# Six DRAM copies moved behind a weight reload, one product's low part moved last, one head's keys loaded map by map

## The chip, the cores and the metric

The kernel runs on one core of one Trainium2 chip. The metric is the device time of one execution in microseconds (us). A core has five engines with a queue of instructions each: TensorE (PE, matmuls and transposes), VectorE (DVE), ScalarE (ACT), GpSimd (POOL) and SyncE (SP), which here only issues DMA transfers. An engine takes its queue in order; semaphores hold an instruction until what it reads is there.

## The reference

One layer of a hybrid decoder, sequence 1024, width 1024, all in fp32. The normalised input `h` is multiplied by one wide matrix; the columns of the product feed differential attention (8 heads, each with two maps of queries and keys of width 64) and gated linear attention (GLA, 4 heads); both results are gated, multiplied by `w_out`, normalised, and added to `x`.

```
h = rms_norm(x, pre_g)
z = h @ w_in
qa, ka, va, ga, qb, kb, vb, gb, gk_low = split_columns(z)
oa = diff_attention(qa, ka, va, lam)      # per block: w = softmax(q1 k1^T) - lam softmax(q2 k2^T); w @ v
oa = rms_norm(oa, subln_g) * (1 - lam_init) * silu(ga)
ob = gla_chunked(qb, kb, vb, log_sigmoid(gk_low @ w_gk_up + b_gk) / 16)
ob = rms_norm(ob, gla_g) * silu(gb)
y = concat([oa, ob]) @ w_out
return x + rms_norm(y, post_g)
```

## The kernel before, in words

**Arithmetic.** TensorE multiplies in a reduced fp32 format, so an operand that must keep its precision is split into a high part (a rounded copy, made by ACT as a CAST) and a low part (the rest, made by DVE as a subtraction). A product is three groups of matmuls that add up in one PSUM bank: high times high, high times low, low times high.

**The first stage** computes `h @ w_in` by pairs of column blocks, each with a seven-product scheme of the Strassen kind on 2 by 2 blocks of h (h11, h12, h21, h22) and of the weights (b11, b12, b21, b22). Products are numbered 1 to 7. Product 1 uses h11, 2 h12, 3 s4, 4 h22, 5 s1, 6 s2, 7 s3, where s1 to s4 are sums and differences of blocks of h. `order` (L270 on) lists steps (pair p, product n). Pairs 0 and 1, called GATED, are the value columns of GLA: they come first, both with the same weights tiles but other columns of h. Step (p, n) works for two units, 128 rows of the output each. So (0, 1) and (1, 1) come first, then (0, 2) and (1, 2), then two steps of pair 2, then (0, 5), (1, 5), (0, 6), (1, 6), (0, 7), (1, 7), (0, 4), (1, 4).

`multiply_values` (L455 to L472) issues such a step. For p in GATED, h is the stationary operand and the weights stream. For n below 3 each unit's chain stands alone: four matmuls with h high and w high (`y<-w,h_hi`), four with h low and w high (`y<-w,h_lo`), four with h high and w low. A weight tile of product n covers two of the four slices k of the inner dimension, so a product has two high tiles and two low tiles.

`step_values` (L548) follows each step with what drains it. After product 6 ACT copies bank x to a tile s (`s<-x`, four copies named s_785, s_787, s_823, s_825 for the four units). After products 2, 4 and 3 DVE adds a bank and such a tile into gv_st (`take_gated`, L523), frees the bank, and two stores of 128 KB on SP's queue (L528) write it out. gv_st has four buffers.

`gated_weights` (L321) makes the weights of a product: DVE subtracts raw blocks (`g_raw<-g_raw`), ACT casts the high part (`w<-g_raw`), DVE subtracts for the low part (`w<-g_raw,w`). The raw blocks are loaded on SP's queue by `load_gated` (L257) and, since b21 is needed a second time when its buffers have been overwritten, by `load_again` (L261 to L266), twice, 512 KB each, into g_raw_651 and g_raw_752. Raw weights of later pairs come through `load_raw` (L218) as w_raw. `parts` (L751) makes the high and low parts of s1, s2, s3, s4, h22 from fp32 tiles t.

After step (1, 4) the main flow computes the low-rank gate input (`low_rank`, L929): PSUM tile gkl_ps takes a bank that a gv_st of the product 2 or 4 stage has freed.

**Attention** runs later, head by head (its score matmuls `sc` stand at 615.8 to 885.4 us). `all_scores` (L1365) walks the query blocks qb from 7 to 0; after block 4 of a head it calls `load_qk` (L1143) for the next head: queries q, keys k and keys with halves exchanged ks, for half 1 and half 0 of the sequence, each map a DMA of 256 KB (q, k, L1152) or two of 128 KB (ks, L1155). `turn` (L1389) transposes the weights of the softmax difference on PE into `wtr`.

**The output stage** `out_early` (L1573) accumulates parts of the final product. At its top of the loop over st, six copies move rows of x into the output, DRAM to DRAM, 16 x 8192 elements or 512 KB each (L1589), to which the last stage adds its result (a DMA with `accum_op`).

**Order.** PE's instructions are pinned to the order of the program. All other engines' instructions are put in order when the program is built, by a scheduler that goes by its own times (`schedule_with_timeline_sim`), within the data dependencies and `tc.issue_after(a)`, which puts what is issued in its scope behind instruction a. The six copies depend on nothing but their input, and the scheduler puts them near the start of SP's queue.

Of the kernel before, what the change touches and what calls it, by code (L numbers as in the profile page):

```python
# [14 lines left out]
P = 128  # L15
# [10 lines left out]
QA, KA, VA, GA, QB, KB, VB, GB, GKL = 0, 1024, 2048, 3072, 4096, 4608, 5120, 6144, 7168  # L26
# [5 lines left out]
def hymba_kernel(  # L32
# [21 lines left out]
    pe, sp = nc.tensor, nc.sync  # L54
# [22 lines left out]
    def fp(t):  # L77
        return t.bitcast(F32)

    def cols(half):  # L80
        return slice(half * 512, half * 512 + 512)
# [61 lines left out]
    def mm(*a, **k):  # L143
        tc.keep_in_program_order(pe.matmul(*a, **k))  # L144
# [25 lines left out]
    def at(part, j):  # L170
        per = HB // len(part)
        return part[j // per][:, j % per]
# [31 lines left out]
    GATED = (0, 1)  # L204
# [45 lines left out]
    def load_gated(name):  # L250
# [4 lines left out]
        for i, r in enumerate(gated_raws[name]):  # L255
            rows = slice(r0 + i * 256, r0 + i * 256 + 256)
            sp.dma_start(r, w_in[0, rows, c0 : c0 + 512].rearrange("(k p) c -> p k c", p=P))  # L257
            if name == "b11" and not i:
                sp.dma_start(pre_g, pre_norm_g[0].rearrange("(k p) -> p k", p=P))

    def load_again(i):  # L261

        r = kp.tile([P, 2, 512], F32, tag=("ks0", "k0")[i], name="g_raw")
        gated_raws.setdefault("b21x", []).append(r)
        rows = slice(512 + i * 256, 512 + i * 256 + 256)
        sp.dma_start(r, w_in[0, rows, VB : VB + 512].rearrange("(k p) c -> p k c", p=P))  # L266

    EARLY = 3
    order = [(0, 1), (1, 1), (0, 2), (1, 2), (2, 1), (2, 2)]
# [185 lines left out]
    def multiply_values(i, pss, start):  # L455

        p, n = order[i]
        hi, lo = H[LEFT[n]]
        w = ws.pop(i)
        def chains(us):  # L460
            for j, (a, b) in enumerate(((0, hi), (0, lo), (1, hi))):
                for k in range(HB):
                    for u in us:
                        c = (p % 2 * 2 + u) * P
                        mm(
                            pss[u], at(b, k)[:, c : c + P], w[a][k // 2][:, k % 2, :],
                            start=(start and j == 0 and k == 0), stop=(j == 2 and k == HB - 1),
                            skip_group_check=True,
                        )

        for us in ((0,), (1,)) if p in GATED and n < 3 else ((0, 1),):
            chains(us)  # L472
# [667 lines left out]
        for st in streams:  # L1140
            yield from st

    def load_qk(h, n, half):  # L1143

        if h % 2 and half == 0 and n != "q":
            t = smps[0].tile([P, 2, 512], F32R, tag=f"{n}0", name=f"{n}0")
        else:
            t = kp.tile([P, 2, 512], F32R, tag=f"{n}{half}", name=f"{n}{half}")
        for m in range(2):
            d = qk_d["q" if n == "q" else "k"][h][m, :, :, cols(half)]  # L1150
            if n != "ks":
                ins = sp.dma_start(fp(t[:, m]), d.rearrange("t p s -> (t p) s"))  # L1152
            else:
                for i in range(2):
                    ins = sp.dma_start(fp(t[64 * i : 64 * i + 64, m]), d[1 - i])  # L1155
        qk_load[:] = [ins.ins]
        qk[h, n, half] = t

    qk, smps, qk_load = {}, [], []
# [8 lines left out]
    for n in ("q", "k", "ks"):  # L1168
        load_qk(0, n, 1)
        if n != "q":  # L1170
            load_qk(0, n, 0)
# [28 lines left out]
    def mix(st):  # L1200

        part = mix_tiles()
        for t in range(2):
            ins = (pool if st == 1 else sp).dma_start(fp(part[t]), mixe[st, t])
            if st < 2:
                tc.keep_in_program_order(ins)
        return part
# [157 lines left out]
    def all_scores():  # L1365
        for h in range(DA_HEADS):
            for qb in range(NT - 1, -1, -1):
                if qb in (3, 5) and h:
                    yield lambda h=h, half=qb // 4: (h - 1, half) in used
                yield from scores(h, qb)  # L1370
                if qb == 4 and h + 1 < DA_HEADS:
                    for n in ("q", "k", "ks"):
                        load_qk(h + 1, n, 1)
                    late = qk_load[0]
                    for n in ("k", "ks"):
                        load_qk(h + 1, n, 0)
                    for t in range(0 if h else 2):
                        with tc.issue_after(late):
                            sp.dma_start(fp(v_first[t])[:, 4:], v_d[0][0, t][:, 4:])
            if h + 1 < DA_HEADS:  # L1380
                load_qk(h + 1, "q", 0)
        scored.append(True)
        opened.update(dict.fromkeys(SC))
# [144 lines left out]
    def load_mix(st, e, n, pool_d=None):  # L1528
        rows = slice(st * P, (st + 1) * P)
        if pool_d:  # L1530
            raw = pool_d.tile([P, 4, P], F32, tag="m_raw", name="m_raw", bufs=4)
        else:
            raw = wop.tile([P, 4, P], F32, tag="m_raw", name="m_raw", bufs=4)
        mix_load[:] = [sp.dma_start(raw[:, :n, :], md[:, e : e + n, rows]).ins]
        return raw
# [20 lines left out]
    def times(ps, part, e0, dh, e, last):  # L1556
        mh, ml = part
        hi, lo = wo[e]
        for i, (a, b) in enumerate(((mh, hi), (ml, hi), (mh, lo))):
            mm(  # L1560
                ps, a[:, e - e0, :], b[:, cols(dh)],
                start=(e == e0 and i == 0), stop=(e == last and i == 2),
            )

    def y_bank(st, dh, name):
        return bank(Y[dh], [P, 512], name)

    def y_tile(ps):
        y = smp.tile([P, 512], F32, tag="yst", name="yst", bufs=2)
        act.copy(y, ps)  # L1570
        return y

    def out_early():  # L1573

        part = mix0
        ps = [y_bank(0, dh, "ypart") for dh in range(2)]
        for e in range(E, E + 8):
            yield 1.0
            if e == E:
                nxt = mix1  # L1580
            for dh in range(2):
                times(ps[dh], part, E, dh, e, E + 7)
            yield 1.0
        for dh in range(2):
            sp.dma_start(yd[0][dh], y_tile(ps[dh]))
        for st in range(1, NT - 1):
            part, nxt = nxt, mix(st + 1)
            rows = slice(ENDS[st - 1] * P, ENDS[st - 1] * P + P)
            sp.dma_start(out[0, rows, :], x[0, rows, :])  # L1589
            for dh in range(2):  # L1590
                ps = y_bank(st, dh, "ypart")
                for e in range(E, E + 8):
                    times(ps, part, E, dh, e, E + 7)
                    yield 0.69
                sp.dma_start(yd[st][dh], y_tile(ps))

        yield lambda: len(stored) >= 7
        part = nxt
        ps = [y_bank(NT - 1, dh, "ypart") for dh in range(2)]
        raws_o = [load_mix(st, 0, 4) for st in ENDS[:3]]  # L1600
        for e in range(E, E + 8):
            for dh in range(2):
                times(ps[dh], part, E, dh, e, E + 7)
                yield 0.69
            if e < E + 4:
                weights(e - E)
            if e == E + 6:
                nxt = mix_part(ENDS[0], 0, 4, raws_o.pop(0))
        for dh in range(2):
            kept = sp.dma_start(yd[NT - 1][dh], y_tile(ps[dh]))  # L1610
        for n, st in enumerate(ENDS):
            part = nxt
            if n == 1:
                yield lambda: len(stored) >= 8
            if n + 3 < NT:
                raws_o.append(load_mix(ENDS[n + 3], 0, 4))

            if 1 <= n <= 4:
                with tc.issue_after(kept.ins), tc.issue_after(mix_load[0]):
                    weights(3 + n)  # L1620
            if n + 1 < NT:
                nxt = mix_part(ENDS[n + 1], 0, 4, raws_o.pop(0))
            for dh in range(2):
                ps = y_bank(st, dh, "ypart")
                for e in range(4):
                    times(ps, part, 0, dh, e, 3)
                    yield 0.69
                pool.dma_start(yd[st][dh], y_tile(ps), accum_op=ALU.add)
        yield lambda: len(stored) >= 2 * (DA_HEADS - 1) - 1
        mix_pair(0)  # L1630
        for n, st in enumerate(ENDS[:2]):
            if n:
                yield lambda: scored
            for dh in range(2):
                seed(st, dh, (Y, SC)[n][dh], sums_of(n)[:, dh])
            yield 0.7
        for st in ENDS[:2]:
            for dh in range(2):
                for e in range(4, 7):
                    last_times(st, dh, parts_d[st], e)  # L1640
                    yield 0.69
            if st == ENDS[0]:
                mix_pair(2)
                seed(ENDS[2], 0, SC[2], sums_of(2)[:, 0])
# [189 lines left out]
```

## Time and profile before

| | |
|---|---|
| time, median of 3 runs | 961.57 us (961.07 to 963.14) |
| the profiled execution's own time | 961.47 us |
| its span in the trace | 959.8 us |
| what lies outside the span | 1.7 us |
| granted TensorE clock, mean | 0.998 |
| busy share of the span, PE, DVE, ACT, POOL | 99%, 77%, 63%, 20% |
| DMA traffic | 220.34 MB, mean 230 GB/s |

All times below count from the start of the span. A row of the timeline has the start, the length (from the first start to the last end, when the row has several), the engine, the line, the operation, the tiles as output<-inputs without buffer numbers, the shapes, the count, and in brackets how long the engine had been idle and what released it. PE's ends are modelled, so a matmul of 512 columns shows about 0.39 us, though the next one starts 0.23 us after it. SPq rows are SP's issuing of DMAs, not the transfers.

### The profile page before, as it was taken

Reading aid. Unit: us, or ns where it says so; the run is one execution under the profiler, and the core shown is the slowest. Engines: PE = TensorE matmul, PEld = TensorE weight load, DVE = VectorE, ACT = ScalarE, POOL = GpSimd, SP = SyncE. Lnnn points to the kernel's source line nnn. Section 1 sums busy time; section 2 is a strip of 40 time slices with the busy share of each in tenths; the row PEclk is TensorE's granted clock in tenths of the full one; section 3 lists DMA queues with packets and bytes.
Section 4 is the critical chain, followed back from the end, with each engine's and each line's share of the span. In section 5 each row is a group of like instructions: output and inputs, shape, how many; then the busy total and the mean of one; then the engine's idle time right before and its main releaser. Section 6 shows DMA issues by size and latency. Waiting matters only on the chain.

```text
span 959.8 us, 14356 instructions
## 1 busy us (share of the span) xinstructions
PE 950.1 (99%) x4624; PEld 792.8 (83%) x4624; DVE 742.7 (77%) x1476; ACT 605.6 (63%) x1162; POOL 193.0 (20%) x263
## 2 busy tenths in 40 slices
PE   9999999999999999999999999999999999999997
PEld 7887788888888888888888888878888888888885
DVE  6998799996778787687758476588888888898464
ACT  7753355745777556577765444366677687787773
POOL 2001002222141112121100002122222222443321
PEclk9999999999999999999999999999999999999999
DMA  9706367487577898986755498996666679994777
GB/s 348 226 23 169 93 202 259 160 294 242 189 254 242 275 298 263 292 277 199 260 175 156 143 298 272 405 290 213 220 220 197 220 228 362 316 293 102 162 206 143
DMA packets 153258, 220.34 MB, mean 230 GB/s; under 512 B 15776, under 2 KB 85664, under 8 KB 153088
## 3 DMA queue, kind: packets, MB, share of 16 engines
q1 hardware_dynamic: 138736, 177.65, 57.9%
q0 software_dynamic: 14448, 41.79, 15.0%
q8 instruction: 36, 0.59, 0.2%
q14 instruction: 38, 0.31, 0.1%
HBM read 133.93 MB, written 88.60 MB: 232 GB/s over the span
## 4 chain that ended last, share of the span: by engine, by line
PE 89%; DVE 5%; DMA 3%; SPq 1%; ACT 1%; issue 0%; DVEq 0%; ACTq 0%
PE x L144 21%; PE z L144 15%; PE y L144 14%; PE ypart L144 13%; PE sc L144 7%; PE po L144 5%; PE yps L144 4%; PE wtr L147 3%; PE gpo L144 3%; DMA g_raw<-in_w_in_dram 2%; PE kv L144 1%; DMA ks<-k_d 1%; DVE s_lo L66 1%; PE gkl_ps L144 1%; PE pa L144 1%; DVE w L66 1%
## 5 line engine op out<-in xcount | busy, mean ns | idle before, releaser
L66 ACT CAST w<-w_raw 128x512 fp32r<-128x512 f32 x138 | 85.4, 621 | 72.7 <-PE y L144 32.2
L66 DVE TENSOR_TENSOR w<-w_raw,w 128x512 fp32r<-128x512 f32 x138 | 94.5, 687 | 32.4 <-ACT w L66 32.2
L66 ACT ACTIVATE p<-p,stt 128x896 f32<-128x896 f32 (+7 forms) x128 | 99.3, 777 | 30.2 <-DVE stt L66 29.2
L66 ACT COPY s<-x 128x512 f32<-128x512 f32 x78 | 44.9, 587 | 68.7 <-PE x L144 68.3
L66 DVE CUSTOM_DVE_ANT_0 p<-sc,maskt 128x512 f32<-128x512 f32 (+3 forms) x128 | 74.3, 585 | 15.3 <-PE sc L144 14.2
L66 POOL TENSOR_SCALAR p<-p,stt,lam 128x1024 f32<-128x1024 f32 (+3 forms) x64 | 56.2, 879 | 144.5 <-DVE stt L66 141.3
L144 PE MATMUL z<-s_hi,w 128*128 128x512 f32 x320 | 80.1, 392 | 0.0
L144 PE MATMUL x<-s_hi,w 128*128 128x512 f32 x320 | 80.0, 392 | 0.0
L144 PE MATMUL y<-h_hi,w 128*128 128x512 f32 x320 | 80.0, 392 | 0.0
L144 PE MATMUL ypart<-wo_hi,m_hi 128*128 128x512 f32 x192 | 79.6, 414 | 0.1
L144 PE MATMUL ypart<-wo_hi,m_lo 128*128 128x512 f32 x192 | 75.5, 393 | 0.0
L144 PE MATMUL ypart<-wo_lo,m_hi 128*128 128x512 f32 x192 | 75.4, 393 | 0.0
L66 POOL DMA_DIRECT2D wo_d<-wo_hi x32 | 17.4, 545 | 269.2 <-ACT wo_hi L66 269.2
L144 PEld LDWEIGHTS z<-s_hi,w 128*128 128x128 f32 x320 | 59.8, 188 | 12.3
L144 PEld LDWEIGHTS x<-s_hi,w 128*128 128x128 f32 x320 | 59.7, 188 | 12.3
L144 PEld LDWEIGHTS y<-h_hi,w 128*128 128x128 f32 x320 | 59.7, 188 | 12.2
L144 PE MATMUL sc<-k,q 128*128 128x512 f32 (+1 forms) x192 | 68.8, 362 | 0.1
L144 PE MATMUL sc<-ks,q 128*128 128x512 f32 (+1 forms) x192 | 66.1, 348 | 0.4 <-DMA ks<-k_d 0.4
L66 ACT CAST wt_hi<-wtr 128x512 fp32r<-128x512 f32 (+1 forms) x80 | 42.8, 536 | 30.7 <-PE wtr L147 29.8
L66 DVE TENSOR_TENSOR wt_lo<-wtr,wt_hi 128x512 fp32r<-128x512 f32 (+1 forms) x80 | 50.6, 633 | 9.9 <-ACT wt_hi L66 9.2
L66 DVE TENSOR_TENSOR c<-z,s 128x512 f32<-128x512 f32 x48 | 32.8, 688 | 31.8 <-ACT s L66 19.6
L66 DVE TENSOR_TENSOR w_raw<-w_raw 128x512 f32<-128x512 f32 x80 | 56.0, 700 | 1.2 <-DMA w_raw<-in_w_in_dram 0.2
(234 smaller groups left out, 2349.1 us busy)
## 6 DMA issues: line engine op xcount, KB each, us to landing
w_raw<-in_w_in_dram SPq DMA_DIRECT2D x40, 512.0 KB, 5.1
wo_d<-wo_hi POOLq DMA_DIRECT2D x32, 256.0 KB, 2.9
q<-q_d SPq DMA_DIRECT2D x32, 256.0 KB, 5.3
k<-k_d SPq DMA_DIRECT2D x32, 256.0 KB, 5.3
ks<-k_d SPq DMA_DIRECT2D x64, 128.0 KB, 6.1
wo_raw<-in_w_out_dram POOLq DMA_DIRECT2D x31, 256.0 KB, 4.8
v<-v_d SPq DMA_DIRECT2D x14, 512.0 KB, 7.5
wo_d<-gqd POOLq DMA_DIRECT2D x22, 256.0 KB, 4.2
```

Of the source, the lines that this page charges most:

```text
L66: ins = op(*a, **k)
L144: tc.keep_in_program_order(pe.matmul(*a, **k))
L147: tc.keep_in_program_order(pe.transpose(dst, src, ident))
```

## The change

Three edits.

1. `load_again` keeps its DMAs in a list, and the six copies of `out_early` stand in the scope of `tc.issue_after(reloads[1])`, that is, behind the second reload (g_raw_752) on SP's queue.
2. In `multiply_values`, for pairs 0 and 1 and product 2, the order of the three groups is high times high, w low times h high, w high times h low, in place of high-high, h low, w low.
3. `load_qk` takes the maps that it is to load; for head 1 alone, `all_scores` calls it for map 0 of q, k, ks half 1 and k, ks half 0, and then for map 1 of the same. The other heads load both maps of one tile after another as before.

```diff
+    reloads = []
     def load_again(i):
...
-        sp.dma_start(r, w_in[0, rows, VB : VB + 512].rearrange("(k p) c -> p k c", p=P))
+        ins = sp.dma_start(r, w_in[0, rows, VB : VB + 512].rearrange("(k p) c -> p k c", p=P))
+        reloads.append(ins.ins)
...
         p, n = order[i]
         hi, lo = H[LEFT[n]]
         w = ws.pop(i)
+        terms = ((0, hi), (0, lo), (1, hi))
+        if p in GATED and n == 2:
+            terms = ((0, hi), (1, hi), (0, lo))
+
         def chains(us):
-            for j, (a, b) in enumerate(((0, hi), (0, lo), (1, hi))):
+            for j, (a, b) in enumerate(terms):
...
-    def load_qk(h, n, half):
-
-        if h % 2 and half == 0 and n != "q":
+    def load_qk(h, n, half, maps=(0, 1)):
+
+        if maps[0]:
+            t = qk[h, n, half]
+        elif h % 2 and half == 0 and n != "q":
...
-        for m in range(2):
+        for m in maps:
...
                 if qb == 4 and h + 1 < DA_HEADS:
-                    for n in ("q", "k", "ks"):
-                        load_qk(h + 1, n, 1)
-                    late = qk_load[0]
-                    for n in ("k", "ks"):
-                        load_qk(h + 1, n, 0)
+                    for maps in ((0, 1),) if h else ((0,), (1,)):
+                        for n in ("q", "k", "ks"):
+                            load_qk(h + 1, n, 1, maps)
+                        late = qk_load[0]
+                        for n in ("k", "ks"):
+                            load_qk(h + 1, n, 0, maps)
...
             rows = slice(ENDS[st - 1] * P, ENDS[st - 1] * P + P)
-            sp.dma_start(out[0, rows, :], x[0, rows, :])
+            with tc.issue_after(reloads[1]):
+                sp.dma_start(out[0, rows, :], x[0, rows, :])
```

The order of the engines' queues, as the build makes it, moves further than these lines: the pieces that matter are shown in the prediction, where a name with a number is one buffer of the program.

## The prediction

> **What bounds the kernel now.** I read the page first, then the waits of PE, then PE's timeline, since its table of waits leaves nearly nothing.
>
> The page's busy times, and PE's waits:
> ```profile
> PE 950.1 (99%) x4624; PEld 792.8 (83%) x4624; DVE 742.7 (77%) x1476; ACT 605.6 (63%) x1162; POOL 193.0 (20%) x263
> ...
> PE spin L144 <- POOL idle L66: 1.5, 1, 1.5
> PE sc L144 <- DMA ks<-k_d: 0.4, 1, 0.4
> PE x L144 <- DVE w L66: 0.2, 1, 0.2
> ```
> PE bounds the kernel: what does not shift its starts costs nothing. But 99% hides small stalls, because the ends are modelled. They show in the spacing of starts. PE's timeline of the first stage:
> ```profile
> 25.50 1.17 PE L144 MATMUL y<-w,h_hi 128*128 128x512 f32 x4
> 26.50 1.76 PE L144 MATMUL y<-w,h_lo 128*128 128x512 f32 x4
> 28.10 2.02 PE L144 MATMUL y<-w,h_hi 128*128 128x512 f32 x8
> ...
> 34.49 2.20 PE L144 MATMUL y<-w,h_hi 128*128 128x512 f32 x8
> 36.54 1.08 PE L144 MATMUL y<-w,h_lo 128*128 128x512 f32 x4
> ...
> 58.28 1.98 PE L144 MATMUL x<-w,s_lo 128*128 128x512 f32 x8
> 60.09 3.79 PE L144 MATMUL x<-w,s_hi 128*128 128x512 f32 x16
> ...
> 65.53 3.79 PE L144 MATMUL x<-w,s_hi 128*128 128x512 f32 x16
> ...
> 70.97 1.07 PE L144 MATMUL x<-w,s_hi 128*128 128x512 f32 x4
> 72.24 3.04 PE L144 MATMUL x<-w,s_hi 128*128 128x512 f32 x12 [0.20 <-DVE w L66]
> ...
> 89.62 2.01 PE L144 MATMUL gkl_ps<-h_hi,wl 128*64 128x512 f32 x8
> ```
> From 58.28 to 60.09 eight matmuls take 1.81, so one takes 0.227 and four 0.91. The four `y<-w,h_lo` from 26.50 take 1.60: 0.69 lost. The eight from 34.49 take 2.05: 0.24 lost. From 25.50 to 26.50 it is 0.09 more; with 0.05 in 28.10's group I count 1.07 up to 38. From 70.97 to 72.24 it is 0.36. DVE's timeline tells what was late:
> ```profile
> 25.22 2.49 DVE L66 TENSOR_TENSOR h_lo<-f,h_hi 128x512 fp32r<-128x512 f32 x4
> ...
> 33.63 1.23 DVE L66 TENSOR_TENSOR g_raw<-g_raw 128x1024 f32<-128x1024 f32 x1 [1.71 <-DMA g_raw<-in_w_in_dram]
> 34.77 0.68 DVE L66 TENSOR_TENSOR gv_st<-y,s 128x512 f32<-128x512 f32 x1
> ...
> 61.53 2.50 DVE L66 TENSOR_TENSOR s_lo<-t,s_hi 128x512 fp32r<-128x512 f32 x4 [0.74 <-ACT s_hi L66]
> ...
> 70.97 1.22 DVE L66 TENSOR_TENSOR w<-g_raw,w 128x1024 fp32r<-128x1024 f32 x1
> ...
> 74.92 1.23 DVE L66 TENSOR_TENSOR g_raw<-g_raw 128x1024 f32<-128x1024 f32 x1 [0.26 <-DMA g_raw<-in_w_in_dram]
> ...
> 81.62 0.69 DVE L66 TENSOR_TENSOR w_raw<-w_raw 128x512 f32<-128x512 f32 x1 [0.21 <-DMA w_raw<-in_w_in_dram]
> ...
> 83.41 1.41 DVE L66 TENSOR_TENSOR w_raw<-w_raw 128x512 f32<-128x512 f32 x2
> 84.74 1.28 DVE L66 TENSOR_TENSOR gv_st<-y,g_raw 128x512 f32<-128x512 f32 x2
> ```
> The low part h_lo is made while PE already wants it (25.22 to 27.71). The bank of 34.49's group is freed by gv_st at 34.77, which stood behind a DVE wait of 1.71 for raw weights. The stall at 72.24 ends with w's low part (70.97 + 1.22 = 72.19).
>
> **The copies.** Before, they are issued ahead of those raw weights. The copies' issues with their times to landing, and SP's timeline:
> ```profile
> L1589 SPq DMA_DIRECT2D out_dram<-in_x_dram x6: 572/588/1067, 18.3 to 22.2; - x6
> ...
> DMA to landing us min/median/max: 5.3/7.5/9.2
> ...
> 24.19 1.51 SPq L257 DMA_DIRECT2D g_raw<-in_w_in_dram  x2
> ...
> 71.11 0.38 SPq L266 DMA_DIRECT2D g_raw<-in_w_in_dram  x1
> 74.55 1.99 SPq L218 DMA_DIRECT2D w_raw<-in_w_in_dram  x2
> ```
> They land from about 18.3 + 5.3 = 23.6 to 22.2 + 9.2 = 31.4: 1.6 apart. The load issued at 24.19 lands at 33.6, after the last. SP's queue, before:
> ```order
> L1589 DMA out_0_dram<-in_x_dram 16x8192 x6
> L257 DMA g_raw_498<-in_w_in_dram 128x2x512
> L257 DMA g_raw_499<-in_w_in_dram 128x2x512
> L266 DMA g_raw_651<-in_w_in_dram 128x2x512
> L528 DMA gv0_d_126<-gv_st_472 128x2x128
> ```
> And after, from the second reload on:
> ```order
> L268 DMA g_raw_752<-in_w_in_dram 128x2x512
> L1600 DMA out_0_dram<-in_x_dram 16x8192 x5
> L218 DMA w_raw_861<-in_w_in_dram 128x4x256
> L1600 DMA out_0_dram<-in_x_dram 16x8192
> L218 DMA w_raw_863<-in_w_in_dram 128x4x256
> L535 DMA gv2_d_128<-gv_st_852 128x2x128
> ```
> So five copies now stand ahead of w_raw_861 and six ahead of w_raw_863. Removed: DVE's 1.71 and with it the 0.24. Added: 9.6 us of copies ahead of w_raw. Who waits: DVE subtracts from w_raw_863 twice, then adds gv_st_958, which frees the bank of gkl_ps. Before, w_raw_863 lands at 81.6 and PE needs the bank at 89.62.
>
> After, g_raw_752 lands at 74.9 + 0.8 (below) = 75.6. What a queued w_raw load takes, from two issued one behind the other elsewhere:
> ```profile
> L218 SPq DMA_DIRECT2D w_raw<-in_w_in_dram x2: 637/770/902, 322.6 to 323.7; - x2
> ...
> DMA to landing us min/median/max: 6.2/6.3/6.4
> ```
> They land at 328.8 and 330.1: 1.3 each. So w_raw_863 lands at 75.6 + 6 x 1.6 + 2 x 1.3 = 87.8, and the bank is free 1.41 + 0.68 later, at 89.9; PE comes at 89.62 + 0.8 = 90.4. Cost nothing, with 0.5 to spare. The other end: in this very place w_raw_861 landed about 78.2 (DVE used it only later) and w_raw_863 at 81.6, 3.4 apart. With 3.4 for each, 92.0 and 94.1: PE waits 3.7. I take the first, as its queue is as full as this one will be. A gain is excluded: nothing waited for these loads on PE.
>
> [...]
>
> **Low part of h last.** Per chain, four matmuls with h high now come first, so `h_lo` is wanted 0.91 later, at 27.4, when three of its four tiles are made and the fourth follows at 27.71, ahead of its own matmul. The 0.69 and the small stalls beside it go; w's low part, wanted earlier, was made before DVE began h_lo at 25.22. With the copies' 0.24, PE is 1.07 earlier at 38.
>
> But ACT's queue is in another order behind that. The difference, on ACT, around the cast of s3 and the copies of product 6's banks (x_332 to x_335):
> ```order
>  L66 CAST s2_hi_625<-s24_620 128x512
> -L66 CAST s3_hi_725<-t21_416 128x512 x4
>  L66 COPY s_785<-x_332 128x512
>  L66 COPY s_787<-x_333 128x512
> +L66 CAST s3_hi_725<-t21_416 128x512 x4
> +L66 COPY s_823<-x_334 128x512
>  L66 CAST w_735<-g_raw_498 128x1024
> +L66 COPY s_825<-x_335 128x512
>  L66 CAST w_736<-g_raw_499 128x1024
> -L66 COPY s_823<-x_334 128x512
> -L66 COPY s_825<-x_335 128x512
> ```
> s3's cast now waits for PE to finish (0, 6), and w_735 for (1, 6). ACT's rows:
> ```profile
> 60.88 2.18 ACT L66 CAST s_hi<-t 128x512 fp32r<-128x512 f32 x4 [5.49 <-DVE h_lo L66]
> 62.97 1.06 ACT L66 COPY s<-x 128x512 f32<-128x512 f32 x2
> 65.20 2.19 ACT L66 CAST w<-g_raw 128x1024 fp32r<-128x1024 f32 x2 [1.17 <-DVE g_raw L66]
> ```
> (0, 6) ends before at 60.09 + 1.82 = 61.91, so now at 60.84, its first bank a matmul earlier, 60.6. Two copies (1.06) to 61.7, and s_lo starts 0.65 after s_hi (61.53 - 60.88): 62.3, where it was 61.53. That is +0.8 for DVE's chain, which shows no idle time from there to 72.19 to give it back: w's low part comes at 73.0. PE on its own road: (1, 6) ended at 65.53 + 1.82 = 67.35 and now at 66.28, x_334 at 66.05; copy 0.53, w_735 1.05: 67.6; copy and w_736: 69.2, where PE before started those k slices at 65.53 + 2.73 = 68.26; twelve matmuls later it is 71.9, and four more 72.8. So PE's saved 1.07 is gone, and w's low part ends the wait: 73.0 against 72.24, **+0.8**. Were PE's saving 0.3 smaller, the copies would come 0.3 later and this would be +1.1; were w's low part not the last, +0.6.
>
> [...]
>
> **Head 1's keys.** Removed: the one wait of PE for ks. Rows of the timeline there:
> ```profile
> 633.79 0.88 DVE L66 SCALAR_TENSOR_TENSOR p<-p,stt,p 128x640 f32<-128x640 f32 x1
> ...
> 634.32 0.39 PE L144 MATMUL ypart<-wo_lo,m_hi 128*128 128x512 f32 x1
> 634.59 0.55 DVE L66 CUSTOM_DVE_ANT_0 p<-sc,maskt 128x384 f32<-128x384 f32 x1
> 634.73 0.66 PE L147 MATMUL wtr<-ident,p 128*128 128x128 f32 x4
> ...
> 640.25 0.40 PE L144 MATMUL sc<-k,q 128*128 128x512 f32 x1
> 641.01 0.47 PE L144 MATMUL sc<-ks,q 128*128 128x512 f32 x1 [0.36 <-DMA ks<-k_d]
> ```
> 640.25 to 641.01 is 0.76 for one matmul: 0.53 lost. Map 0's ks now has the map 1 pieces of q and k behind it, two transfers of 256 KB, so it lands over 1 us earlier and the 0.53 goes. But on DVE a score step now stands ahead of the mix that PE's wtr waits for:
> ```order
> -L66 SCALAR_TENSOR_TENSOR p0_5948<-p0_5948,stt_5947,p1_5847 128x640
>  L66 ISA p0_6021,stt_6020<-sc_6023,maskt_79 128x384
>  L66 ISA stt_6020 128x1
> +L66 SCALAR_TENSOR_TENSOR p0_5948<-p0_5948,stt_5947,p1_5847 128x640
> ```
> The mix comes 0.55 + 0.09 later (0.6), and wtr already waited for it. Net -0.53 + 0.6 = **+0.1**, between -0.5 (if DVE is early enough) and +0.4.
>
> **The sum**, against the profiled execution: 961.47 + 0.8 + 0 + 0.1 = **962.4**. That execution lies 0.10 under the median of the runs. About 0.2%, 1.9 us, is what a measurement of this kernel can tell from no change: 959.65 to 963.49.
>
> **Rivals.**
>
> R1, all stalls gone. If ACT's copies do not hold s3 up, since DVE's lost 1.71 lets the whole chain move forward, then -1.07 - 0.36 - 0.53: 961.47 - 2.0 = 959.5. For it: the 1.71 really goes. Against: the cast stands behind the copies, whatever DVE does. 0.08.
>
> R2, slower: the copies hold up w_raw_863, and PE waits for gkl_ps's bank. It decides from a landing at 89.4 (1.6 later than worked out: bank at 91.5, PE at 90.4, +1.1 and the +0.9 make 2.0). With 3.4 per load: 961.47 + 0.9 + 3.7 = 966.1. For it: six copies on one queue held the load of 24.19 up to 33.6; against: 0.5 spare and the 1.3. 0.20. [...]
>
> R3, no net change: ACT holds nothing up, w's low part stays at 72.19 and swallows PE's 1.07; attention cancels. 961.5. It needs s3's cast at its old time, so 0.15.
>
> **The numbers.** Forecast 0.57, R3 0.15, R2 0.20, R1 0.08. Faster is R1, 0.08; slower is R2, 0.20; same 0.72. The range, 960.2 to 964.6, holds forecast and R3 with their bounds (the +0.6 with -0.5 gives 961.6, the +1.1 with +0.4 963.0) the way down to R1 by half, and the nearer half of R2; it leaves out R1 and about 0.1 of R2.
>
> **What would show it.** DVE's 1.71 wait gone, `y<-w,h_lo` four in 0.91, s_hi<-t behind two s<-x at about 61.7, and the third PE group of (0, 7) at about 73.0. PE's gkl_ps at 90.4 for me, from 91.5 for R2. No ks wait at 640, a longer one at wtr. Wrong if PE reaches 72 early (R1), if gkl_ps waits more than 1 us (R2), or if another stage's stall moves by over 1 us.

## The result, and the profile after

The changed kernel takes 963.88 us (median of 15 runs, 963.38 to 965.70), the kernel before 961.60 (15 runs, 960.81 to 963.41). The ratio is 1.0024, with a 95% interval of 1.0016 to 1.0032: 2.3 us slower, between 1.5 and 3.1. That is inside the range forecast and 1.5 above the forecast itself; it is the sign of rival R2, but, as the trace shows, not its mechanism.

The profiled execution of the changed kernel takes 963.6 us with a span of 961.7. First the waits of PE, of which the kernel before had three:

```profile
PE x L144 <- ACT w L66: 1.6, 2, 1.4
...
PE wtr L147 <- DVE p L66: 0.6, 1, 0.6
PE sc L144 <- DVE stt L66: 0.3, 1, 0.3
```

The ks wait and the wait for w's low part are gone. In their place stand a wait for ACT's weights (x <- ACT w) and two in attention (wtr, sc). The two rows left out belong to the start: spin with 1.5, as before, and xT with 0.7, of which more below. PE's timeline in the first stage:

```profile
26.08 2.07 PE L144 MATMUL y<-w,h_hi 128*128 128x512 f32 x8
27.99 1.07 PE L144 MATMUL y<-w,h_lo 128*128 128x512 f32 x4
28.90 1.98 PE L144 MATMUL y<-w,h_hi 128*128 128x512 f32 x8
...
37.05 1.07 PE L144 MATMUL y<-w,h_lo 128*128 128x512 f32 x4
...
65.13 1.98 PE L144 MATMUL x<-w,s_hi 128*128 128x512 f32 x8
68.50 1.20 PE L144 MATMUL x<-w,s_hi 128*128 128x512 f32 x4 [1.39 <-ACT w L66]
69.93 1.20 PE L144 MATMUL x<-w,s_hi 128*128 128x512 f32 x4 [0.24 <-ACT w L66]
70.97 2.00 PE L144 MATMUL x<-w,s_lo 128*128 128x512 f32 x8
72.81 4.02 PE L144 MATMUL x<-w,s_hi 128*128 128x512 f32 x16
...
89.36 1.98 PE L144 MATMUL y<-w,h_hi 128*128 128x512 f32 x8
91.17 2.00 PE L144 MATMUL gkl_ps<-h_hi,wl 128*64 128x512 f32 x8
```

The low part of h now costs its 0.91 (27.99 to 28.90). The 48 matmuls and 8 transposes of product 2 in this stretch take 26.08 to 37.05 + 0.91 = 37.96, that is 11.88, where they took 25.50 to 36.54 + 1.82 = 38.36, that is 12.86: 0.98 saved. Then, from 65.13 + 1.82 = 66.95 to 68.50, PE stands still for 1.55, and before 69.93 for another 0.52 (68.50 to 69.93 is 1.43, and four matmuls take 0.91). At gkl_ps nothing is lost: 89.36 to 91.17 is 1.81, the plain pace of eight matmuls.

The copies' issues in the changed kernel, with their times to landing:

```profile
L1600 SPq DMA_DIRECT2D out_dram<-in_x_dram x6: 575/588/1439, 73.1 to 76.9; - x6
...
DMA to landing us min/median/max: 5.4/8.1/10.8
```

From 73.1 + 5.4 = 78.5 to 76.9 + 10.8 = 87.7 land six copies and, between the last two in SP's order, the first raw weight (76.35 + 10.1 = 86.5; DVE takes it at 86.48): 1.5 each.

ACT and then DVE of the changed kernel there:

```profile
61.47 1.07 ACT L66 COPY s<-x 128x512 f32<-128x512 f32 x2 [5.85 <-PE x L144]
62.43 2.19 ACT L66 CAST s_hi<-t 128x512 fp32r<-128x512 f32 x4
66.91 0.59 ACT L66 COPY s<-x 128x512 f32<-128x512 f32 x1 [2.29 <-PE x L144]
67.39 1.05 ACT L66 CAST w<-g_raw 128x1024 fp32r<-128x1024 f32 x1
```

```profile
58.53 2.49 DVE L66 TENSOR_TENSOR h_lo<-t,h_hi 128x512 fp32r<-128x512 f32 x4
63.10 2.50 DVE L66 TENSOR_TENSOR s_lo<-t,s_hi 128x512 fp32r<-128x512 f32 x4 [2.07 <-ACT s_hi L66]
...
72.53 1.22 DVE L66 TENSOR_TENSOR w<-g_raw,w 128x1024 fp32r<-128x1024 f32 x1
...
89.10 1.30 DVE L66 TENSOR_TENSOR w_raw<-w_raw 128x512 f32<-128x512 f32 x2 [0.55 <-DMA w_raw<-in_w_in_dram]
90.31 0.69 DVE L66 TENSOR_TENSOR gv_st<-y,g_raw 128x512 f32<-128x512 f32 x1
```

ACT idles 5.85 us in front of a copy that waits for PE, with s3's cast behind it; DVE's wait for s_hi grows from 0.74 to 2.07. Product 7's first weight is cast at 67.39 to 68.44, behind the copy of a bank that PE has only just filled, and PE starts on it at 68.50. s3's cast is held by the queue alone: before, it started 0.09 behind DVE's h_lo (58.30 + 2.49 = 60.79, cast at 60.88); now h_lo ends at 58.53 + 2.49 = 61.02, and the cast starts at 62.43, right behind two copies. That is 1.41 behind h_lo where it was 0.09: in this trace the cast, though h_lo was done, did not pass the two copies ahead of it in ACT's queue, for the first of which ACT waited until 61.47.

PE in attention, where the ks wait was:

```profile
635.51 0.45 PE L144 MATMUL sc<-k,q 128*128 128x384 f32 x1 [0.35 <-DVE stt L66]
...
637.40 0.66 PE L147 MATMUL wtr<-ident,p 128*128 128x128 f32 x4 [0.57 <-DVE p L66]
```

Comparing the same matmul in the two traces, in order of time: +0.53 by 10 us (the third load of x landed later, ACT starts on it at 7.93 instead of 7.38; none of the edits stands that early in a queue), -0.97 by 36, +1.53 at 67, +0.64 at 68.5, -0.22 at 72, nothing until 633, +0.56 and +0.54 at 633 to 637, -0.60 at 641; the sum is +2.0, and nothing worth naming follows. Without the start that is +1.5. The matmul of 10 us stands between 9.95 and 11.1 in the profiles of all the kernels of this study, before and experiments alike, so I take its 0.53 for the spread of single executions; the 2.3 of the medians is compatible with 1.5, at the edge of its interval.

### The profile page after: what moved, and what is told of

Its sections match the earlier page's. It is cut to its first block, busy times and chain, and to the rows that moved or that the text cites. A ratio compares the mean times of both kernels' runs of the same rounds, so it can differ in the third digit from the quotient of the medians.

```text
span 961.7 us, 14359 instructions
## 1 busy us (share of the span) xinstructions
PE 949.6 (99%) x4624; PEld 792.7 (82%) x4624; DVE 742.5 (77%) x1476; ACT 605.1 (63%) x1162; POOL 195.5 (20%) x263
## 4 chain that ended last, share of the span: by engine, by line
PE 96%; ACT 1%; DVE 1%; DMA 1%; issue 0%; POOL 0%; SPq 0%; DVEq 0%; ACTq 0%; POOLq 0%
PE x L144 24%; PE z L144 16%; PE y L144 16%; PE ypart L144 13%; PE sc L144 7%; PE po L144 5%; PE yps L144 4%; PE wtr L147 3%; PE gpo L144 3%; PE kv L144 1%; PE gkl_ps L144 1%; PE pa L144 1%; DMA x<-in_x_dram 1%; PE xT L147 1%; DVE p L66 0%
```

## Experiments

The theories. Mine: edits 1 and 3 are harmless or gain; edit 2 gains 1 us itself, but makes the build put other instructions ahead on ACT (first stage) and on DVE (attention), and these cost over 2 us. The rival: the six copies hold up loads (R2).

### The three edits, each alone

Copies alone (edit 1), low part last alone (edit 2), keys alone (edit 3): each is the kernel before with one of the three parts of the diff above, unchanged.

> Only the copies are moved behind the second reload; the other two edits are undone. ACT keeps the order of before (s3's cast ahead of the copies of product 6). My theory (the loss comes from the engines' orders behind the low-part edit, the moved copies are harmless): DVE's wait of 1.71 us for raw weights goes, PE's 0.24 goes, part of the 0.36 at 72 us, gkl_ps does not wait; 0.2 to 0.6 us faster than before, about 961.2. Rival (the six copies hold the loads behind them up): PE waits for gkl_ps or later work, 1.5 us or more slower than before, about 963.1 or above.

> Only the low part of h is moved last in the two steps; copies and keys as before. The build then puts ACT's product 6 copies ahead of s3's cast, as in the changed kernel, and DVE's reciprocal and mix in attention behind score steps. My theory: PE gains 0.7 to 0.8 by 38 us, loses about 2.0 between 66 and 74 us to ACT's order, and about 0.6 net in attention; 1.5 to 2.0 us slower than before, about 963.3. Rival (the copies cost it): 0 to 0.8 us faster than before, about 961.2.

> Only head 1's queries and keys are loaded map by map; no engine but SP changes its order. My theory: PE's wait for ks at 641 us goes and nothing takes its place; 0.5 us faster than before, about 961.1. Rival (the reload order itself makes DVE's mix late, or moves the wait to another piece): no gain, 961.6 or up to 0.5 slower.

Measured, against 961.24 us for the kernel before on the same chip: copies alone 961.06 (ratio 0.9996, 0.9988 to 1.0005), low alone 963.19 (1.0021, 1.0012 to 1.0029), keys alone 961.08 (0.9998, 0.9989 to 1.0007). Only edit 2 is slower, by 1.95, and by the same mechanism. PE's waits with the low part alone:

```profile
PE x L144 <- ACT w L66: 1.6, 2, 1.4
...
PE wtr L147 <- DVE p L66: 0.6, 1, 0.6
PE sc L144 <- DVE stt L66: 0.4, 1, 0.4
```

The waits for ACT w, wtr and sc are all there, with the copies and the keys where they were. With the keys alone, ACT, DVE and POOL run the same instructions in the same order as before; so the reordering of attention on DVE, which I had put down to the keys, belongs to the low part too. An edit at 25 us moved rows at 630 us; that the build's own times carry the shift on is likely, but not shown. The gains of copies and keys alone are within the uncertainty; in their traces the 1.71 us wait of DVE (copies) and the ks wait of PE (keys) are gone. But two things speak against counting these waits as gains of those edits. With the copies alone DVE now makes both raw subtractions ahead of gv_st, and PE loses 0.48 at 32.81 waiting for that bank, while 0.2 of the 0.24 at 34.49 is saved. And the ks wait is gone also with the low part alone, where the keys are loaded as before: 642.43 to 642.67 is 0.24 for the matmul that took 0.76.

### ACT's order kept

The changed kernel, with product 6's copies held behind s3's last cast (pair 0) and behind product 7's weight cast (pair 1). Its core:

```diff
+                first6 = casts.get(p) if n == 6 and gated else None
-                with tc.issue_after(act.last) if k == "s1" else nullcontext():
+                with tc.issue_after(act.last) if k == "s1" else (
+                    tc.issue_after(first6) if first6 else nullcontext()
+                ):
                     act.copy(b[k], b["x"])
```

(casts[0] is the last cast of s3's high parts, casts[1] that of product 7's weights.)

> All three edits, but ACT's copies of product 6 are held behind s3's casts (pair 0) and behind product 7's weight casts (pair 1), as they stood before; the build then leaves DVE's order in attention as before too. My theory: the loss of 2.0 us at 66 to 74 goes, w's low part on DVE is then the last to come (its 0.36 stays or grows), attention gains its 0.5; 0.5 to 1.4 us faster than before, about 960.6, and 3 us faster than the changed kernel. Rival (copies or start-up cost it): still 1.5 us or more slower than before, about 963.1.

Measured: 960.62 against 961.24 (0.9995, 0.9986 to 1.0004), 0.6 faster than before, which is within the uncertainty, where the changed kernel is 2.3 slower. With ACT's order held the build also leaves DVE, ACT and POOL in attention (600 to 700 us) in the order of before, so this kernel undoes both reorderings: the loss comes from the two of them together, and the next experiment parts them. PE's timeline at 70:

```profile
70.25 1.07 PE L144 MATMUL x<-w,s_hi 128*128 128x512 f32 x4
72.09 3.06 PE L144 MATMUL x<-w,s_hi 128*128 128x512 f32 x12 [0.78 <-DVE w L66]
```

70.25 to 72.09 is 1.84 for four: 0.93 lost, where it was 0.36 before. PE brings its saved time to 70 and loses 0.57 of it to w's low part, which is R3's point. DVE in the same kernel:

```profile
43.11 0.69 DVE L66 TENSOR_TENSOR s_lo<-s,s_hi 128x512 fp32r<-128x512 f32 x1 [0.26 <-ACT s_hi L66]
45.00 0.69 DVE L66 TENSOR_TENSOR c<-y,s 128x512 f32<-128x512 f32 x1 [0.60 <-PE y L144]
55.27 0.69 DVE L66 TENSOR_TENSOR s_lo<-s,s_hi 128x512 fp32r<-128x512 f32 x1 [0.69 <-ACT s_hi L66]
...
61.38 2.50 DVE L66 TENSOR_TENSOR s_lo<-t,s_hi 128x512 fp32r<-128x512 f32 x4 [0.74 <-ACT s_hi L66]
```

Of the 1.71 that DVE no longer waits for raw weights, 0.26, 0.60 and 0.69 came back as other waits, and s_lo starts at 61.38 against 61.53. That is the order of this kernel, not a rule: with the copies alone s_lo starts at 60.55, 0.98 earlier than before. How much of a removed wait reaches the end of a queue depends on the inputs that stand in between.

### Attention's order kept

The changed kernel with ACT as it is; in attention the reciprocal of head 0's block 5 is held ahead of block 4's last score steps and block 2's score step behind block 4's mix.

```diff
-                forced = (h, qb) == (0, NT - 2) or (h, qb, m) == (0, 3, 0)
+                forced = (h, qb) == (0, NT - 2) or (h, qb, m) in ((0, 3, 0), (0, 2, 0), (0, 4, 1))
...
-                    if (h, qb) == (0, 4):
+                    if (h, qb) in ((0, 4), (0, 5)):
                         lowest[:] = [rec.ins]
...
+                        if (h, qb) == (0, 4):
+                            lowest[:] = [mixed_one.ins]
```

> All three edits, ACT's order as in the changed kernel (product 6's copies ahead of s3's cast), but in head 0's attention DVE's reciprocal of block 5 is held ahead of the last map's score steps of block 4, and the score step of block 2 behind the mix of block 4, as before. My theory (two separate reorderings cost): PE still loses 1.0 us net by 74 us, the 1.1 us at 633 to 637 go; 0.5 us slower than before, about 1.1 us faster than the changed kernel. Rival (ACT's order costs it all, the attention rows only take up slack): as the changed kernel, 2 us or more slower than before.

Measured: 962.20 against 961.36 (1.0015, 1.0006 to 1.0024): 0.84 slower than before, 1.4 less than the changed kernel. Of the 0.84, 0.44 is lost at 145 us, in a place where neither the kernel before nor the changed one loses anything; why is not shown. The fourth case, ACT's order as before and attention's as in the changed kernel, was not run. Both waits of attention are gone, and ACT's stands:

```profile
PE x L144 <- ACT w L66: 1.6, 2, 1.4
PE spin L144 <- POOL idle L66: 1.5, 1, 1.5
```

The table has these two rows only. What the wait for sc was shows in POOL's rows and DVE's. The changed kernel:

```profile
631.81 1.93 POOL L66 TENSOR_SCALAR p<-p,stt,lam 128x768 f32<-128x768 f32 x1 [3.05 <-DVE stt L66]
...
631.48 0.16 DVE L66 RECIPROCAL stt<-stt 128x2 f32<-128x2 f32 x1
...
631.81 1.15 DVE L66 SCALAR_TENSOR_TENSOR p<-p,stt,p 128x896 f32<-128x896 f32 x1
633.77 1.02 DVE L66 SCALAR_TENSOR_TENSOR p<-p,stt,p 128x768 f32<-128x768 f32 x1 [0.81 <-POOL p L66]
```

And POOL with attention's order kept:

```profile
631.07 0.99 POOL L66 TENSOR_SCALAR p<-p,stt,lam 128x768 f32<-128x768 f32 x1 [2.62 <-DVE stt L66]
```

The reciprocal, put behind score steps, releases POOL at the very moment at which DVE starts a mix. POOL's step takes 1.93 instead of 0.99, DVE waits 0.81 for it with its next mix, and the score steps behind that free PE's banks late.

### Are the copies behind the reload free?

The kernel with ACT's order kept, but with the copies pinned to the place in SP's queue that they have in the program, in the output stage:

```diff
             with tc.issue_after(reloads[1]):
-                sp.dma_start(out[0, rows, :], x[0, rows, :])
+                tc.keep_in_program_order(sp.dma_start(out[0, rows, :], x[0, rows, :]))
```

> As the kernel with ACT's order kept, but the six copies are pinned to where the program has them, in the output stage, so that none stands ahead of the weight loads at 72 to 89 us. My theory (six copies behind the reload fit into slack of 0.1 to 0.5 us): no difference from the kernel with ACT's order kept within 0.3 us. Rival (they hold up loads there): 0.5 us or more faster than that kernel. A loss here would mean that copies in the output stage collide with its loads.

Measured: 960.69 against 961.36 (0.9993, 0.9985 to 1.0002), 0.67 faster than before where the one with copies behind the reload was 0.62 faster. So no cost of the six copies is seen there. How near they are to costing: in the changed kernel gv_st_958 ends at 90.31 + 0.69 = 91.00, and PE takes its bank at 91.17.

Then more of them. The kernel with ACT's order kept, and nine further copies into spare DRAM behind the reload (work that nothing uses):

```diff
         reloads.append(ins.ins)
+        for k in range(9 if i else 0):
+            spare_d = tc.dram_tile([16, 8192], F32, name=f"spare{k}_d")
+            with tc.issue_after(ins.ins):
+                sp.dma_start(spare_d, x[0, k % 8 * P : k % 8 * P + P, :].rearrange("(a b) c -> a (b c)", a=16))
```

> As the kernel with ACT's order kept, with nine more copies of 512 KB from x to a spare DRAM tensor right behind the second reload, ahead of the loads of raw weights (extra work, no result of the kernel changes). The build then puts the six copies behind those loads and DVE's gv_st ahead of the subtractions. My theory (a queue in order at 1.6 us for each copy): the second raw weight lands at about 94 instead of 88, PE waits 2 to 3 us for the weights of pair 2's product 5 at about 93; 2.4 us slower than the kernel with ACT's order kept. Rival (the loads are served beside the copies): no difference.

Measured: 964.81 against 961.36 (1.0041, 1.0027 to 1.0054; five runs): 3.45 slower than before, 4.1 slower than the kernel with ACT's order kept, more than the 2.4 expected, and by another road. PE and DVE of this kernel:

```profile
88.27 1.98 PE L144 MATMUL y<-w,h_hi 128*128 128x512 f32 x8
92.66 3.48 PE L144 MATMUL gkl_ps<-h_hi,wl 128*64 128x512 f32 x8 [2.42 <-DVE gv_st L66]
95.98 2.00 PE L144 MATMUL gkl_ps<-h_lo,wl 128*64 128x512 f32 x8
...
91.82 0.69 DVE L66 TENSOR_TENSOR gv_st<-y,g_raw 128x512 f32<-128x512 f32 x1 [9.55 <-DMA gv_d<-gv_st]
```

gkl_ps waits for its bank after all, as R2 has it, yet not through the raw weights: DVE waits 9.55 us for a free gv_st buffer, whose store stands behind the copies. The build also changed attention's order again here (waits for wtr 0.6 and sc 0.3), so the 4.1 is not one term. Comparing its trace with that of ACT's order kept, PE loses 3.9 at the bank (2.6 of wait, the rest in the eight matmuls behind it, on which more below) and 1.4 in attention; but this profile lies 1.9 above the median of its runs, and how much of the 4.1 is the bank stays open.

### Making use of it

With ACT's order kept, w's low part ends the wait at 72. DVE makes s4's low parts between product 7's two low weights, though s4 is needed only later:

```diff
             w_lo(0)
+            w_lo(1)
         for j in range(2 * i, 2 * i + 2):
             behind = [parts("s4", j, s24[i][:, j % 2], None if i else lows[7])]
         if not i:
             load_again(1)
-            with tc.issue_after(behind[0].ins):
-                w_lo(1)
```

> As the kernel with ACT's order kept, but DVE makes the second low part of product 7's weights ahead of the low parts of s4. My theory (w's low part ends the wait at 72 us and swallows the saved time): that wait of 0.8 us goes, the second reload comes 1.2 us later and gives back up to 0.3 at product 4; 0.5 to 0.8 us faster than the kernel with ACT's order kept, about 1.2 faster than before. Rival (another wait takes its place): no faster than the kernel with ACT's order kept.

Measured: 960.00 against 961.36 (0.9985, 0.9976 to 0.9994): 1.36 faster than before, 0.7 more than with ACT's order alone, which the two intervals don't tell apart. PE's timeline and a row of DVE's, where the wait moves to product 4's second weight:

```profile
70.23 3.79 PE L144 MATMUL x<-w,s_hi 128*128 128x512 f32 x16
...
77.49 1.07 PE L144 MATMUL y<-w,h_hi 128*128 128x512 f32 x4
78.94 1.21 PE L144 MATMUL y<-w,h_hi 128*128 128x512 f32 x4 [0.38 <-ACT w L66]
79.99 2.01 PE L144 MATMUL y<-w,h_lo 128*128 128x512 f32 x8
...
76.58 1.23 DVE L66 TENSOR_TENSOR g_raw<-g_raw 128x1024 f32<-128x1024 f32 x1 [0.84 <-DMA g_raw<-in_w_in_dram]
```

The wait at 72 is gone; but the eight from 77.49 take 2.50 instead of 1.81, so 0.69 is given back where up to 0.3 was expected. ACT's weight there waits for DVE's subtraction, and that for the second reload.

The same without edit 2, in two steps. Copies and keys alone together, and then with the low weights first:

```diff
-        terms = ((0, hi), (0, lo), (1, hi))
-        if p in GATED and n == 2:
-            terms = ((0, hi), (1, hi), (0, lo))
-
...
-            for j, (a, b) in enumerate(terms):
+            for j, (a, b) in enumerate(((0, hi), (0, lo), (1, hi))):
```

> The first and third edit without the second (copies behind the reload, head 1's keys map by map, the low part of h in its old place). My theory (the low-part edit alone, through the orders that the build makes behind it, turns the change into a loss): ACT and DVE in attention keep their order of before, PE's ks wait and the 0.24 at 34 us go; 0.3 to 1.0 us faster than before, 2.5 us or more faster than the changed kernel. Rival (the edits cost together what none costs alone): within 0.2 us of before, or slower.

> As the kernel with the copies and the keys alone, and DVE makes the second low part of product 7's weights ahead of s4's low parts, the low part of h in its old place. My theory: the stall of 0.36 us at 72 goes, but the 0.7 of the low part of h is not there to be kept; 0.2 to 0.4 us faster than the kernel with copies and keys, 0.3 to 0.8 slower than the one with all three edits, ACT's order kept and low weights first. Rival (the low part of h was hidden anyway): as fast as that one.

Measured, against 961.53: copies and keys 960.33 (0.9988, 0.9979 to 0.9997), with low weights first 960.43 (0.9988, 0.9979 to 0.9997). So edits 1 and 3 without edit 2 are 1.2 us faster than before, 3.5 better than all three (1.2 and 2.3, each against the kernel before beside it): edit 2 turned a gain into the loss. The low weights first give nothing without edit 2 (expected 0.2 to 0.4), a miss. PE's timeline with copies and keys alone says why:

```profile
32.67 1.21 PE L144 MATMUL y<-w,h_hi 128*128 128x512 f32 x4 [0.25 <-DVE gv_st L66]
...
69.09 1.98 PE L144 MATMUL x<-w,s_lo 128*128 128x512 f32 x8
70.90 3.79 PE L144 MATMUL x<-w,s_hi 128*128 128x512 f32 x16
```

The sixteen from 70.90 go through in 3.79, the length of sixteen without a wait: the stall of 0.36 that the low weights were to take away was gone with the copies' move already, since PE, held up for a bank at 32.67, comes no earlier while DVE does: DVE ends w's low part at 69.90 + 1.22 = 71.12, and PE wants it at 70.90 + 0.91 = 71.81.

Last, the best of what was learnt: all three edits, ACT's order kept, low weights first, and the copies in the output stage. The diff is those of ACT's order, of the late copies and of the low weights together.

> All three edits, ACT's order kept, low weights of product 7 first, and the six copies pinned to the output stage. My theory (the copies behind the reload cost nothing, the wait of 0.4 us at 79 is for the second reload itself, which goes out 1.2 us later here): within 0.3 us of the same kernel with the copies behind the reload, 1.2 us faster than before. Rival (the copies delay that reload or the weights behind it): 0.4 us or more faster than that kernel.

Measured: 959.63 against 961.53 (0.9983, 0.9975 to 0.9992), 1.9 faster than before, the fastest kernel of the study, 4.2 us under the changed one (1.9 and 2.3). The difference of 0.5 to the one with copies behind the reload (1.36) is inside both intervals, so the times don't decide between the theory (within 0.3) and the rival (0.4 or more). The trace leans to the rival:

```profile
77.11 2.32 PE L144 MATMUL y<-w,h_hi 128*128 128x512 f32 x8
79.27 1.08 PE L144 MATMUL y<-w,h_lo 128*128 128x512 f32 x4
```

The eight take 2.16, so 0.35 is lost where it was 0.69. The second reload landed sooner where no copies followed it: 3.7 us from its issue in the kernel before and 4.0 in the changed one, 3.6 to 4.0 in all five kernels without them, 4.0 to 4.4 in the eight with copies behind it. So the copies seem to delay the reload ahead of them too, by a few tenths. With the low weights first PE waits for the reload, and 0.3 is at stake; in the changed kernel and with ACT's order alone kept it does not, and nothing is.

## Why the prediction was right or wrong

**The low part last: right.** 1.07 forecast for it and the copies' 0.24 together, 0.98 in the trace. The low part alone already brings 0.95 by the same comparison of matmuls, so the copies' 0.24 is not seen as a term of its own.

**ACT's order: right in mechanism, short in size.** +0.8 net at 72 forecast, +1.04 in the trace (1.57 - 0.53). I had x_334 copied a matmul before (1, 6) ends; ACT starts that copy at 66.91, just as PE ends (66.95), so that w's first cast ends at 68.44 where my sum, shifted by the start's 0.53, gave 68.15. PE then reached w's second low part at 72.81 + 0.91 = 73.72, and DVE had it at 72.53 + 1.22 = 73.75: the two roads came out together, where I had PE's 0.2 ahead. The kernel with ACT's order kept shows this to be the cause: there the matmul that was +1.57 late starts at 72.09, 0.15 earlier than before. And with attention's order kept ACT's wait stays, and so does a loss, of 0.84.

**The copies: right.** Forecast nothing, by a landing at 87.8 with 0.5 to spare; in the trace w_raw_863 was used at 89.10, 0.8 later than forecast after the shift of the start, and 0.17 was to spare. Most of the 0.8 is the reload itself, which landed at 72.7 + 4.0 = 76.7 (75.6 forecast, 76.1 with the start), the term that I took over from before. PE's plain pace at gkl_ps shows that it cost nothing, and the kernel with late copies agrees. R2 is rejected for six copies, and shown as a real danger for more of them.

**Head 1's keys: the step that failed.** I took DVE's mix behind a score step for a consequence of the keys and priced it at 0.6 against 0.53. The keys alone do not move DVE; the low part does. And I looked at the mix alone, not at the reciprocal ahead of it, which holds POOL. Attention came out at +0.56 + 0.54 - 0.60 = +0.5 instead of +0.1, and the two stalls together are over the 1 us that the prediction had named as a sign of being wrong. Nor is the 0.60 shown to be the keys' gain, since the low part alone brings most of it.

**The sum.** +0.9 forecast; +1.5 in the traces without the start (+1.04, 0, +0.5), +2.3 between the medians. What is left of 0.8 lies within the measurement's interval (1.5 to 3.1) and isn't settled. The mechanism's own upper bound was 963.0; 963.88 lies beyond it, in the part of the range that was there for R2, so that the range holds it is partly luck. The chances were too sure of no difference: slower by over 0.2% had 0.20 and came about, with the point on the boundary (0.24%), by the main forecast's own mechanism a little larger, not by R2. R1's argument, that DVE's 1.71 would carry on, fails in DVE's rows with ACT's order kept, where 0.15 of it arrives; with the copies alone 0.98 does. R3's, that w's low part swallows the saved time, holds for more than half of it once ACT's order is repaired.

## What to carry to other kernels

Where a build orders the engines, an edit is costed by what it does to every engine's queue, to the end of the program, and not by its own lines: here an exchange of two groups of matmuls gained what it should (0.98) and lost three times that (1.95 at 67 to 72 us, 1.10 in attention) in rows that nobody had touched. A saved wait is worth what the next-latest input leaves of it (of DVE's 1.71, 0.15 with ACT's order kept and 0.98 with the copies alone); follow the chain to the first place at which PE again waits for something that has not become earlier. When an edit loses, test its parts alone before it is given up: two of the three parts gained 1.2 us together, and the third, with one order held, no longer cost anything that the runs show. That its own 1 us is kept is not shown: with low weights first, the kernel with it is 1.36 faster than before and the one without it 1.10, inside both intervals.

## What the runs showed of the hardware

A POOL step of 128x768 that started together with a two-input DVE step of 1.15 us took 1.93 us (changed kernel, 631.81), and 0.99 in the kernel before (629.63) and with attention's order kept (631.07), where no such step started with it: it was longer by 0.94, most of DVE's step. Of the other seven POOL steps of this shape in the changed kernel, six took 0.98 to 1.00, and one 1.29: that one started at 839.46, while a DVE subtraction of two inputs ran until 839.09 + 0.69 = 839.78. What makes POOL's step longer, the traces do not show.

A wait of 2.42 us of PE cost more than itself. Granted clock by stretches, in the kernel with nine more copies:

```profile
core 0: us, PE busy (x) PEld busy (x) DVE busy (x) ACT busy (x) POOL busy (x), PEclk, DMA share, GB/s
80.00:89.00 9.00, 9.00 (x42) 7.44 (x41) 2.27 (x7) 0.31 (x1) 1.61 (x4) 1.00 0.95 302
89.00:92.60 3.60, 1.24 (x6) 0.70 (x4) 0.78 (x2) 0.00 (x0) 0.54 (x3) 0.97 1.08 364
92.60:96.00 3.40, 3.34 (x9) 1.85 (x10) 3.26 (x6) 0.00 (x0) 0.00 (x0) 0.53 1.17 364
96.00:100.00 4.00, 4.00 (x19) 2.91 (x18) 3.96 (x8) 1.26 (x3) 0.00 (x0) 1.00 0.93 346
```

For 3.4 us behind the wait the granted clock was 0.53, with 0.97 in the stretch ahead and 1.00 in the one behind, and the eight matmuls took 3.32 (92.66 to 95.98), where the changed kernel's take 1.84 (91.17 to 93.01). So the clock fell in the stretch in which PE's last matmul ahead of the wait ended (89.00 + 1.24 = 90.24), and it was back by 96.00. Behind the changed kernel's wait of 1.39 at 68.50 the clock stayed at 1.00 (its stretch from 68 to 71). This is one execution of each, and what makes the clock drop is not shown.
